# Products of probabilities and values per head pair and key source, key block by key block over all queries

## The chip, the cores and the metric

The kernel runs on one core of a Trainium2 chip. The metric is the time of one execution in device microseconds (us). The median of three runs of the kernel before is 1021.41 us (1021.05 to 1021.64).

## What is computed

One layer of a decoder trunk over 512 positions (four query tiles of 128) with a model width of 1024, in 32-bit floats. After a norm and one combined projection, three attention branches A, B and C run over the same positions, are gated, merged and projected, and a feed-forward part follows. Cut to what matters here:

```
A, B, C:  p = softmax(q @ k^T * scale + bias, causal / selected / windowed)
A:  o = p @ v                                   8 heads, one shared v
B:  o = g0*pc @ vcmp + g1*ps @ vs + g2*pw @ vw   8 heads in 2 groups; gates are folded into p
C:  o = (near p) @ v0 + (two dilated p) @ v1, v2   4 output heads, one common softmax
x = x + (sig(gA)*(oA @ W_a) + sig(gB)*(oB @ W_b) + sig(gC)*(oC @ W_c)) @ W_out
x = x + SwiGLU(norm(x))
```

In B the key sources ps and pw cover the same 512 keys here (si = 0 and 1 in the code), and the compressed source pc has 32 keys.

## The kernel before

TensorE (PE) does everything with matrices. The large products (projections, gates, merges, feed-forward) are split into a rounded high part and a low part and done as three float32r matmuls (L106 to L108, mm3). The attention runs beside them: `tick()` advances a generator that emits one step of a software pipeline between pieces of the projections, and the framework's scheduler then sets each engine's order from emission order and its own estimate. Engines run their own rows in that fixed order.

A unit of A or B is one head pair, one query tile i, and in B one key source si. Its step a computes scores of both heads (lg, L363 and L364), adds the bias table on VectorE (DVE, L531), takes the exponential on ScalarE (ACT, L546) and normalises on DVE (L547, L548). Step b transposes the probabilities p on PE, key block by key block (tr, L111, `transposed`), and ACT copies the result to SBUF as pT (L527). Step c multiplies values and probabilities: for key blocks b_ = 0..i and heads j = 0, 1 one matmul with a 128x64 stationary block of v and 128 moving columns of pT, into rows 64j..64j+63 of the PSUM tile ov (L658, L710, in C L874). A head pair has one ov; B adds two more matmuls per query tile for the compressed source (L662), C adds 32 small ones at the end (L882). `head_out` then splits ov into high and low parts (ACT L81, DVE L82) as the tile oT, from which the merge products read.

Column-split matmuls are those whose stationary block has 64 or 32 columns: the two heads of a pair use the two halves of PE's columns. A plain float32 matmul is two records in the trace; a transpose and a float32r matmul are one.

There are two PSUM tiles for scores (lg), two for transposes (tr), one for ov, three for the large products (pm). `ready(bi)` (L997) calls tick until a branch's four oT tiles exist; while it does, no new gate or merge products are emitted.

Of the kernel before, what the change touches and what calls it, by code (L numbers as in the profile page):

```python
# [11 lines left out]
F32 = mybir.dt.float32  # L12
# [8 lines left out]
S = 512  # L21
D = 1024
NT = S // 128
# [44 lines left out]
def block_kernel(ctx: ExitStack, tc: tile.TileContext, x, norm1_g, norm2_g, w_in, qk_norm_g, cmp_pos, cmp_w,  # L68
                 w_ba, w_bb, w_bc, w_out, w_fi, w_fo, rel_bias, onehot, masks, out):
    nc = tc.nc  # L70
# [448 lines left out]
        proj_tm([(C_BQ + 256 * c, 256)], lambda t, ps: nc.scalar.copy(q_tm[:, t, :], ps[:, 0:256]), then=then)  # L519


    def transposed(p, n):
        ps = tr_tile()
        for b in range(n):
            transpose(ps[:, b, :], p[:, b * 128:(b + 1) * 128])
        pt = ap_.tile([128, 4, 128], F32, name="pT", tag="pT", bufs=6)
        nc.scalar.copy(pt[:, 0:n, :], ps[:, 0:n, :])  # L527
        return pt

    def add_table(dst, lg, tab, init, m):  # L530
        nc.vector.tensor_tensor_reduce(out=dst, in0=lg, in1=tab, scale=-1.0, scalar=init, op0=ALU.add, op1=ALU.min,  # L531
# [53 lines left out]
    def cmp_scores(g):  # L585

        def a():
            lg = lg_tile()
            for j in range(4):
                nc.tensor.matmul(lg[32 * j:32 * j + 32, :], kcs[:, 32 * g:32 * g + 32], bq[4 * g + j].bitcast(F32),  # L590
                                 start=True, stop=True)
            sT = ap_.tile([128, S], F32, name="cmpT", tag="p", bufs=5)
            nc.scalar.copy(sT, lg)
            cs_[g] = sT

        return [a]

    def cmp_unit(g, i):
        d = {}

        def a():
            ps = tr_tile()
            transpose(ps[:, 0, :], cs_[g][:, 128 * i:128 * i + 128])
            lg = ps.rearrange("p k c -> p (k c)")
            p = ab.tile([128, 4, 32], F32, name="pc", tag="pc", bufs=2)
            m = ty.tile([128, 8], F32, name="mc", tag="mc")
            nc.vector.tensor_tensor(out=p, in0=lg[:, 0:128].rearrange("p (h n) -> p h n", n=32),
                                    in1=cmask[:, 32 * i:32 * i + 32].unsqueeze(1).to_broadcast([128, 4, 32]), op=ALU.add)
            nc.vector.tensor_reduce(out=m[:, 0:4], in_=p, op=ALU.max, axis=AX.X)
            nc.vector.tensor_tensor(out=p, in0=p, in1=m[:, 0:4].unsqueeze(2).to_broadcast([128, 4, 32]),  # L610
                                    op=ALU.subtract)
            nc.scalar.activation(p, p, AF.Exp)
            nc.vector.tensor_reduce(out=m[:, 4:8], in_=p, op=ALU.add, axis=AX.X)
            nc.vector.reciprocal(m[:, 4:8], m[:, 4:8])
            nc.vector.tensor_tensor(out=m[:, 4:8], in0=m[:, 4:8], in1=bg4[:, i, 4 * g:4 * g + 4, 0], op=ALU.mult)
            nc.vector.tensor_tensor(out=p, in0=p, in1=m[:, 4:8].unsqueeze(2).to_broadcast([128, 4, 32]), op=ALU.mult)
            d["p"] = p

        def b():
            ps = tr_tile()  # L620
            transpose(ps[:, 0, :], d["p"].rearrange("p h n -> p (h n)"))
            pt = ab.tile([128, 128], F32, name=f"pcT{g}_{i}")
            nc.scalar.copy(pt, ps[:, 0, :])
            pcs[g, i] = pt

        return [a, b]

# [2 lines left out]
    def b_units():  # L630
        for pr in range(4):
            hs = (2 * pr, 2 * pr + 1)
            g = pr // 2
            d = {}
            for i in range(NT):
                for si in range(2):
                    yield b_unit(pr, hs, g, i, si, d)

    def b_unit(pr, hs, g, i, si, d):
        u = {}  # L640
        qcol = slice(i * 128, (i + 1) * 128)

        def a():
            if i == 0 and si == 0:
                d["tab"] = [bias_table(8 + h) for h in hs]
            u["p"] = [causal_probs(bq[h], i, bk[si][g], d["tab"][j], None, bg4[:, i, h, si + 1:si + 2])
                      for j, h in enumerate(hs)]

        def b():
            u["pt"] = [transposed(p, i + 1) for p in u["p"]]  # L650
# [36 lines left out]

    def a_unit(pr, i, d):
        u = {}
        qcol = slice(i * 128, (i + 1) * 128)  # L690

        def a():
            if i == 0:
                d["tab"] = [bias_table(2 * pr + j) for j in range(2)]
            if i == 1 and pr < 3:
                a_load(pr + 1)
            if i == 3 and pr < 3:
                a_query(pr + 1)
            u["p"] = [causal_probs(aq[pr][j], i, st_["ak"], d["tab"][j], topm[i], None) for j in range(2)]

        def b():
            u["pt"] = [transposed(p, i + 1) for p in u["p"]]

        def c():
            if i == 0:
                d["ov"] = pvp.tile([128, S], F32, name="ova", tag="pv")
            ov = d["ov"]
            for b_ in range(i + 1):
                for j in range(2):
                    nc.tensor.matmul(ov[64 * j:64 * j + 64, qcol], av[:, b_, :], u["pt"][j][:, b_, :],  # L710
                                     start=(b_ == 0), stop=(b_ == i))
            if i == NT - 1:
                oA.append(head_out(ov))

        return [a, b, lambda: None, c]


    dC = dp.tile([6, 128, NT, 256], F32, name="dC")
# [95 lines left out]
    def c_unit(hf, i, j, ld, d):  # L814
# [30 lines left out]
        def b():  # L845
            ps = tr_tile()
            p = u["p"]
            for b_ in range(w0 // 128):
                transpose(ps[:, b_, :], p[:, 128 * b_:128 * b_ + 128])
            if i < 2:  # L850
                transpose(ps[:, 2, :], p[:, w0 + 2 * n - 128:w0 + 2 * n])
            else:
                for g in range(2):
                    transpose(ps[0:n, 2 + g, :], p[:, w0 + g * n:w0 + g * n + n])
            pt = ap_.tile([128, 4, 128], F32, name="pT", tag="pT", bufs=6)
            nc.scalar.copy(pt[:, 0:w0 // 128, :], ps[:, 0:w0 // 128, :])
# [6 lines left out]
            d[i, j] = pt  # L863

        def c():
            if j == 0:
                return
            if i == 0:
                d["ov"] = pvp.tile([128, S], F32, name="ovc", tag="pv")
            ov = d["ov"]  # L870
# [5 lines left out]
            if i == NT - 1:  # L876
                ovr = ov.rearrange("p (i r w) -> p r i w", i=NT, r=4)
                for g in (1, 2):
                    for r in range(4):
                        for jj in range(2):  # L880
                            h = slice(64 * jj, 64 * jj + 64)
                            nc.tensor.matmul(ovr[h, r], ld["v", g][:, r, h], ld["pt", jj][:, g - 1, :, 32 * r:32 * r + 32],  # L882
                                             start=False, stop=(g == 2 and r == 3))
                oC.append(head_out(ov, unperm=True))

        return [a, b, c]

    def attention():
        yield from pipeline(ab_units())
# [264 lines left out]
```

## Time and profile before

| what | value |
| --- | --- |
| median of three runs | 1021.41 us |
| the profiled execution | 1021.53 us |
| its span in the trace | 1019.7 us |
| PE busy | 1004.5 us (99%) |
| DVE / ACT / POOL busy | 560.3 / 440.2 / 174.8 us |
| PE clock granted | 1.00 |

The span is the time from the first to the last traced instruction; 1.8 us of the profiled execution lie outside it. A matmul's end is modelled, so on PE the steps from start to start are read, not the durations.

### The profile page before, as it was taken

To read this page: it belongs to the slowest core of one execution; us is meant where nothing else is said; L and a number is where in the kernel's file an instruction comes from. 1 tells how busy PE (TensorE), PEld (TensorE's weight loads), DVE (VectorE), ACT (ScalarE), POOL (GpSimd) and SP (SyncE) were. 2 spreads that over 40 slices of the span, in tenths; PEclk is the share of its full clock that TensorE was granted. 3 is DMA by queue.
4 is the path that set the end of the run, shared out by engine and by line. 5 is a ranking of instruction groups with operands and counts; after the bars stand their busy time and mean duration, and the time that the engine had idled before them with its cause. 6 is when DMAs were issued, how large, how long until landed. Compare 5 with 4: busy or idle time off the path is not lost.

```text
span 1019.7 us, 16838 instructions
## 1 busy us (share of the span) xinstructions
PE 1004.5 (99%) x6247; PEld 847.0 (83%) x6247; DVE 560.3 (55%) x1277; ACT 440.2 (43%) x956; POOL 174.8 (17%) x156
## 2 busy tenths in 40 slices
PE   6999999999999999999999999999999999999998
PEld 6799999798887777777777889998888888888886
DVE  7699998555554565554676554553443443432321
ACT  5544555555555555554553433442332332322220
POOL 4226556234100022221010213100000000000000
PEclk9999999999999999999999999999999999999999
DMA  9442244233132333335742353233243333332421
GB/s 212 111 125 53 80 136 130 83 112 98 61 94 82 84 113 105 99 109 156 213 150 83 103 186 115 84 109 98 83 111 96 85 112 94 89 108 94 137 79 42
DMA packets 119267, 109.96 MB, mean 108 GB/s; under 512 B 19931, under 2 KB 105234, under 8 KB 119186
## 3 DMA queue, kind: packets, MB, share of 16 engines
q1 hardware_dynamic: 116994, 107.85, 36.4%
q10 hardware_dynamic: 2192, 1.05, 0.4%
q8 instruction: 49, 0.80, 0.3%
q14 instruction: 32, 0.26, 0.1%
HBM read 96.66 MB, written 12.21 MB: 107 GB/s over the span
## 4 chain that ended last, share of the span: by engine, by line
PE 93%; DMA 3%; SPq 1%; DVE 1%; issue 1%; ACT 0%; POOL 0%; DVEq 0%; ACTq 0%; POOLq 0%
PE pf L108 13%; PE pf L107 13%; PE pf L106 13%; PE pm L107 12%; PE pm L108 12%; PE pm L106 12%; PE tr L111 5%; PE ovb L658 3%; PE lg L363 2%; PE lg L364 2%; PE ova L710 2%; DMA raw<-in_w_in 1%; SPq L246 1%; PE ovc L874 1%; PE lg L829 1%
## 5 line engine op out<-in xcount | busy, mean ns | idle before, releaser
L82 DVE TENSOR_TENSOR wlo<-raw,whi 128x512 fp32r<-128x512 f32 (+1 forms) x243 | 178.5, 741 | 156.1 <-ACT whi L81 151.5
L81 ACT CAST whi<-raw 128x512 fp32r<-128x512 f32 (+1 forms) x288 | 176.6, 618 | 182.1 <-PE pf L108 78.6
L107 PE MATMUL pm<-wlo,xh 128*128 128x256 f32 (+1 forms) x512 | 145.8, 287 | 0.3 <-DVE wlo L82 0.3
L108 PE MATMUL pm<-whi,xl 128*128 128x256 f32 (+1 forms) x512 | 145.1, 285 | 0.5 <-POOL xl L82 0.5
L106 PE MATMUL pm<-whi,xh 128*128 128x256 f32 (+1 forms) x512 | 144.7, 286 | 0.6 <-ACT bgt L374 0.6
L107 PE MATMUL pf<-xl,whi 128*128 128x512 f32 (+1 forms) x384 | 142.6, 372 | 0.1
L106 PE MATMUL pf<-xh,whi 128*128 128x512 f32 (+1 forms) x384 | 142.5, 372 | 0.0
L108 PE MATMUL pf<-xh,wlo 128*128 128x512 f32 (+1 forms) x384 | 142.0, 371 | 0.0
L107 PEld LDWEIGHTS pm<-wlo,xh 128*128 128x128 f32 x512 | 98.1, 192 | 2.3 <-issue 1.2
L108 PEld LDWEIGHTS pm<-whi,xl 128*128 128x128 f32 x512 | 98.1, 192 | 1.6 <-POOL xl L82 0.8
L106 PEld LDWEIGHTS pm<-whi,xh 128*128 128x128 f32 x512 | 97.8, 192 | 1.1 <-ACT bgt L374 0.9
L106 PE MATMUL pm<-xh,whi 128*128 128x512 f32 x224 | 89.1, 398 | 0.0
L108 PE MATMUL pm<-xh,wlo 128*128 128x512 f32 x224 | 89.1, 398 | 0.0
L107 PE MATMUL pm<-xl,whi 128*128 128x512 f32 x224 | 88.9, 397 | 0.0
L82 POOL TENSOR_TENSOR wlo<-raw,whi 128x512 fp32r<-128x512 f32 x45 | 62.9, 1415 | 130.4 <-ACT whi L81 119.8
L107 PEld LDWEIGHTS pf<-xl,whi 128*128 128x128 f32 x384 | 72.3, 188 | 12.7 <-DVE xl L82 0.3
L108 PEld LDWEIGHTS pf<-xh,wlo 128*128 128x128 f32 x384 | 72.2, 188 | 12.6
L106 PEld LDWEIGHTS pf<-xh,whi 128*128 128x128 f32 x384 | 72.2, 188 | 12.3
L106 PE MATMUL pf<-whi,hh 128*128 128x512 f32 x176 | 69.4, 395 | 0.0
L108 PE MATMUL pf<-whi,hl 128*128 128x512 f32 x176 | 69.4, 395 | 0.0
L107 PE MATMUL pf<-wlo,hh 128*128 128x512 f32 x176 | 69.4, 395 | 0.0
L527 ACT COPY pT<-tr 128x128 f32<-128x128 f32 (+3 forms) x96 | 40.7, 426 | 62.6 <-PE tr L111 62.3
(312 smaller groups left out, 1768.2 us busy)
## 6 DMA issues: line engine op xcount, KB each, us to landing
raw<-in_w_in SPq DMA_DIRECT2D x92, 256.0 KB, 3.1
raw<-in_w_ffn_in SPq DMA_DIRECT2D x88, 256.0 KB, 2.8
raw<-in_w_ffn_out SPq DMA_DIRECT2D x44, 256.0 KB, 2.7
raw<-in_w_in SPq DMA_DIRECT2D x52, 128.0 KB, 2.5
x<-in_x SPq DMA_DIRECT2D x8, 512.0 KB, 5.8
tab<-dvec SPq DMA_DIRECT2D x16, 256.0 KB, 3.4
dz<-tz SPq DMA_DIRECT2D x16, 256.0 KB, 2.9
tz<-dz SPq DMA_DIRECT2D x16, 256.0 KB, 2.9
```

What stands on the lines that cost most here:

```text
L81: nc.scalar.copy(dst_hi, src)
L82: (eng or nc.vector).tensor_tensor(out=dst_lo, in0=src, in1=dst_hi.bitcast(F32), op=ALU.subtract)
L106: nc.tensor.matmul(ps, ah, bh, start=(j == 0), stop=False)
L107: nc.tensor.matmul(ps, ah, bl, start=False, stop=False)
L108: nc.tensor.matmul(ps, al, bh, start=False, stop=(j == n - 1))
L111: nc.tensor.transpose(dst, src, ident[0:src.shape[0], 0:src.shape[0]])
L246: nc.sync.dma_start(dst, src)
L363: nc.tensor.matmul(lg, qs, k[:, 0, 0:w], start=True, stop=False)
L364: nc.tensor.matmul(lg, qs, k[:, 1, 0:w], start=False, stop=stop)
L527: nc.scalar.copy(pt[:, 0:n, :], ps[:, 0:n, :])
L658: nc.tensor.matmul(ov[64 * j:64 * j + 64, qcol], bv[si][:, b_, 64 * g:64 * g + 64], u["pt"][j][:, b_, :], start=(si == 0 and b_ == 0), sto ...
L710: nc.tensor.matmul(ov[64 * j:64 * j + 64, qcol], av[:, b_, :], u["pt"][j][:, b_, :], start=(b_ == 0), stop=(b_ == i))
```

## The change

Step c of A, B and C runs once per key source of a head pair, after the last query tile's probabilities have been copied, and not per query tile. For each key block b it multiplies the value block with all queries from tile b on: 512, 384, 256 and 128 moving columns for b = 0..3 (in C 256, 256, 256 and 128). For that the transposed probabilities of all four query tiles lie in one tile per head (13 blocks of 128x128, in C 7), ordered so that the blocks of one key block are neighbours; the copy L530 writes block by block into it. There are four such tiles where there were six of four blocks. In B the loop over key sources is now outside the loop over query tiles, and the compressed probabilities of a group are one tile, so that their product is one matmul of 512 columns per head. The scratch for descriptors of dynamic DMAs is set to 1024 bytes; the kernel's own DMAs are issued from SP and ACT.

```diff
-    def transposed(p, n):
+    def pt_tile(n):
+        return ap_.tile([128, n, 128], F32, name="pT", tag="pT", bufs=4)
+    def transposed(pt, p, i):
         ps = tr_tile()
-        for b in range(n):
+        for b in range(i + 1):
             transpose(ps[:, b, :], p[:, b * 128:(b + 1) * 128])
-        pt = ap_.tile([128, 4, 128], F32, name="pT", tag="pT", bufs=6)
-        nc.scalar.copy(pt[:, 0:n, :], ps[:, 0:n, :])
-        return pt
+        nc.scalar.copy(pt[:, i:4 * i + 1:3, :], ps[:, 0:i + 1, :])
+    def weighted_values(ov, v, pts, first, last):
+        for b in range(NT):
+            for j in range(2):
+                nc.tensor.matmul(ov[64 * j:64 * j + 64, 128 * b:S], v(b), pts[j][:, 4 * b:3 * b + NT, :],
+                                 start=first and b == 0, stop=last and b == NT - 1)
...
-            for i in range(NT):
-                for si in range(2):
+            for si in range(2):
+                for i in range(NT):
                     yield b_unit(pr, hs, g, i, si, d)
...
         def c():
-            if i == 0 and si == 0:
+            if si == 0:
                 d["ov"] = pvp.tile([128, S], F32, name="ovb", tag="pv")
             ov = d["ov"]
-            for b_ in range(i + 1):
-                for j in range(2):
-                    nc.tensor.matmul(ov[64 * j:64 * j + 64, qcol], bv[si][:, b_, 64 * g:64 * g + 64],
-                                     u["pt"][j][:, b_, :], start=(si == 0 and b_ == 0), stop=False)
+            weighted_values(ov, lambda b_: bv[si][:, b_, 64 * g:64 * g + 64], u["pt"], si == 0, False)
             if si == 1:
                 for j in range(2):
-                    nc.tensor.matmul(ov[64 * j:64 * j + 64, qcol], vcp[:, hs[j], :], pcs[g, i], start=False, stop=True)
-                if i == NT - 1:
-                    oB.append(head_out(ov))
-        return [a, b, c]
+                    nc.tensor.matmul(ov[64 * j:64 * j + 64, :], vcp[:, hs[j], :], pcs[g].rearrange("p i q -> p (i q)"),
+                                     start=False, stop=True)
+                oB.append(head_out(ov))
+        return [a, b, c] if i == NT - 1 else [a, b]
...
-        return [a, b, lambda: None, c]
+            ov = pvp.tile([128, S], F32, name="ova", tag="pv")
+            weighted_values(ov, lambda b_: av[:, b_, :], d["pt"], True, True)
+            oA.append(head_out(ov))
+        return [a, b, lambda: None, c] if i == NT - 1 else [a, b]
...
-            for b_ in range(w0 // 128):
-                for jj in range(2):
-                    h = slice(64 * jj, 64 * jj + 64)
-                    nc.tensor.matmul(ov[h, 128 * i:128 * i + 128], ld["v", 0][:, k0 // 128 + b_, h], d[i, jj][:, b_, :],
-                                     start=(i == 0 and b_ == 0), stop=False)
+            for b_ in (0, 2, 1, 3):
+                q1 = min(b_ + 2, NT)
+                for jj, h in enumerate(hs):
+                    nc.tensor.matmul(ov[h, 128 * b_:128 * q1], ld["v", 0][:, b_, h], d["pt", jj][:, 2 * b_:b_ + q1, :],
+                                     start=b_ == 0, stop=False)
...
-    nc = bacc.Bacc("TRN2", target_bir_lowering=False, num_devices=1)
+    nc = bacc.Bacc("TRN2", target_bir_lowering=False, num_devices=1, dynamic_dma_scratch_size=1024)
```

The new names are L530 (copy of pT), L536 (`weighted_values`), L540 and L555 (table and exponential), L670 (compressed source), L876 (C).

PE, end of branch B before (lg_4509 and later are the first scores of A; p_4442 and p_4451 are the last probabilities of B):

```order
L111 MATMUL tr_4491<-ident_82,p_4442 128x128 x4
L363 MATMUL lg_4509<-kst_823,qst_4477 128x128
L364 MATMUL lg_4509<-kst_823,qst_4477 128x128
L111 MATMUL tr_4498<-ident_82,p_4451 128x128 x4
L658 MATMUL ovb_4121<-pT_4496,bv1_888 64x128
L363 MATMUL lg_4518<-kst_823,qst_4480 128x128
L364 MATMUL lg_4518<-kst_823,qst_4480 128x128
L363 MATMUL lg_4562<-kst_823,qst_4477 128x256
L364 MATMUL lg_4562<-kst_823,qst_4477 128x256
L111 MATMUL tr_4552<-ident_82,p_4512 128x128
L658 MATMUL ovb_4121<-pT_4503,bv1_888 64x128
L658 MATMUL ovb_4121<-pT_4496,bv1_888 64x128
```

The same place on PE now (p_4278 and p_4287 are the last probabilities of B, lg_4275 and lg_4284 their scores four rows further up, aq_in the queries of A):

```order
L111 MATMUL tr_4228<-ident_82,p_4181 128x128 x2
L111 MATMUL tr_4265<-ident_82,p_4235 128x128 x3
L111 MATMUL tr_4270<-ident_82,p_4244 128x128 x3
L111 MATMUL tr_4308<-ident_82,aq_in_4263 128x128 x4
L111 MATMUL tr_4319<-ident_82,p_4278 128x128 x4
L111 MATMUL tr_4325<-ident_82,p_4287 128x128 x4
L536 MATMUL ovb_4152<-pT_4161,bv1_888 64x512
L363 MATMUL lg_4335<-kst_823,qst_4313 128x128
L364 MATMUL lg_4335<-kst_823,qst_4313 128x128
L536 MATMUL ovb_4152<-pT_4162,bv1_888 64x512
L536 MATMUL ovb_4152<-pT_4161,bv1_888 64x384
L536 MATMUL ovb_4152<-pT_4162,bv1_888 64x384
```

Six groups of transposes now follow each other with no other product between them; one product of 512 columns stands alone, and the other seven of the key source and the two compressed ones follow in one stretch.

ACT at that place before (the last exponentials of B stand eight rows further up):

```order
L527 COPY pT_4437<-tr_4432 128x512
L320 ACTIVATE qst_4477<-tr_4472,gain8_91 64x512
L320 ACTIVATE qst_4480<-tr_4472,gain8_91 64x512
L527 COPY pT_4496<-tr_4491 128x512
L546 ACTIVATE p_4512,m_4513<-p_4512,m_4513 128x128
L527 COPY pT_4503<-tr_4498 128x512
```

ACT there now, from the last exponentials of B on:

```order
L555 ACTIVATE p_4278,m_4279<-p_4278,m_4279 128x512
L530 COPY pT_4161<-tr_4265 128x3x128
L555 ACTIVATE p_4287,m_4288<-p_4287,m_4288 128x512
L530 COPY pT_4162<-tr_4270 128x3x128
L320 ACTIVATE qst_4313<-tr_4308,gain8_91 64x512
L530 COPY pT_4161<-tr_4319 128x4x128
L320 ACTIVATE qst_4316<-tr_4308,gain8_91 64x512
L530 COPY pT_4162<-tr_4325 128x4x128
```

The exponentials, the copies and A's first queries now alternate, and each copy frees one of the two tr tiles. ACT's rows are the same in number as before.

PE at the end of branch A now (p_5254 and p_5265 are the last probabilities of A):

```order
L363 MATMUL lg_5260<-kst_823,qst_5000 128x512
L364 MATMUL lg_5260<-kst_823,qst_5000 128x512
L111 MATMUL tr_5244<-ident_82,p_5218 128x128 x3
L111 MATMUL tr_5287<-ident_82,p_5254 128x128 x4
L111 MATMUL tr_5293<-ident_82,p_5265 128x128 x4
L536 MATMUL ova_5377<-pT_5137,av_248 64x512
L111 MATMUL tr_5408<-ident_82,c_in_5283 128x128 x4
L536 MATMUL ova_5377<-pT_5138,av_248 64x512
```

Here too no large product stands between the last scores and the transposes that need them. Before, between the same scores (lg_5495) and their transposes there were 21 large products (pm_5830, pm_5909), of which the first six stand here:

```order
L363 MATMUL lg_5495<-kst_823,qst_5217 128x512
L364 MATMUL lg_5495<-kst_823,qst_5217 128x512
L108 MATMUL pm_5830<-oT_4870,wlo_5727 128x512
L106 MATMUL pm_5830<-oT_5147,whi_5726 128x512
L107 MATMUL pm_5830<-oT_5147,whi_5726 128x512
L108 MATMUL pm_5830<-oT_5147,wlo_5727 128x512
L106 MATMUL pm_5830<-oT_5419,whi_5732 128x512
L107 MATMUL pm_5830<-oT_5419,whi_5732 128x512
L111 MATMUL tr_5478<-ident_82,p_5448 128x128 x3
```

The large products that filled this piece of PE's row now stand ahead of it.

Over the whole order, PE's products of probabilities and values (L658, L662, L710, L874, L882) stood in 108 unbroken stretches, 332 matmuls in all; now (L536, L670, L876, L882) they stand in 36, with 152 matmuls.

## Rows read from the trace of the kernel before

**Rows 1.** The page: PE's busy time, and the chain by engine.
```profile
PE 1004.5 (99%) x6247; PEld 847.0 (83%) x6247; DVE 560.3 (55%) x1277; ACT 440.2 (43%) x956; POOL 174.8 (17%) x156
...
PE 93%; DMA 3%; SPq 1%; DVE 1%; issue 1%; ACT 0%; POOL 0%; DVEq 0%; ACTq 0%; POOLq 0%
```
**Rows 2.** Windows of B, A, C: length, busy PE, PEld, DVE, ACT, POOL; clock, DMA.
```profile
180.00:358.00 178.00, 177.14 (x1345) 149.11 (x1344) 98.09 (x305) 99.10 (x266) 32.07 (x24) 1.00 0.29 86
358.00:467.00 109.00, 108.91 (x601) 81.84 (x601) 59.72 (x159) 55.95 (x132) 24.25 (x24) 1.00 0.39 113
467.00:566.00 99.00, 98.02 (x753) 73.79 (x754) 60.88 (x162) 46.20 (x97) 11.50 (x9) 1.00 0.47 140
```
**Rows 3.** PE's groups by line and shape: busy, mean ns | idle.
```profile
L658 PE MATMUL ovb<-pT,bv 128*64 128x128 f32 x320 | 36.8, 286 | 0.0
...
L662 PE MATMUL ovb<-pcT,vcp 128*64 128x128 f32 x64 | 9.7, 276 | 0.0
...
L710 PE MATMUL ova<-pT,av 128*64 128x128 f32 x160 | 18.9, 290 | 0.0
...
L874 PE MATMUL ovc<-pT,c_v 128*64 128x128 f32 x56 | 7.6, 292 | 0.0
```
**Rows 4.** Timeline of PE (start, duration) around a stretch of one matmul.
```profile
462.32 0.40 PE L107 MATMUL pm<-xl,whi 128*128 128x512 f32 x1
462.65 0.43 PE L710 MATMUL ova<-pT,av 128*64 128x128 f32 x2
463.01 0.66 PE L111 MATMUL tr<-ident,c_in 128*128 128x128 f32 x4
463.43 0.47 PE L108 MATMUL pm<-xh,wlo 128*128 128x512 f32 x1
463.74 0.39 PE L106 MATMUL pm<-xh,whi 128*128 128x512 f32 x1
463.97 0.40 PE L107 MATMUL pm<-xl,whi 128*128 128x512 f32 x1
```
**Rows 5.** Timeline of PE around a stretch of seven matmuls.
```profile
465.22 1.09 PE L710 MATMUL ova<-pT,av 128*64 128x128 f32 x14
466.24 0.66 PE L111 MATMUL tr<-ident,c_in 128*128 128x128 f32 x4
```
**Rows 6.** Timeline of PE around L590 (512 columns, 32-column blocks): four matmuls, then one.
```profile
127.92 1.07 PE L590 MATMUL lg<-qst,kcs 128*32 128x512 f32 x8
128.91 0.39 PE L107 MATMUL pm<-wlo,xh 128*128 128x256 f32 x1
...
182.49 1.05 PE L590 MATMUL lg<-qst,kcs 128*32 128x512 f32 x2
183.47 0.43 PE L658 MATMUL ovb<-pT,bv 128*64 128x128 f32 x2
```
**Rows 7.** Chain of waits: four transposes in a row (start, time).
```profile
476.24 0.44 PE tr L111 x4
```
**Rows 8.** ACT's groups by line and shape: busy, mean ns | idle, releaser.
```profile
L546 ACT ACTIVATE p<-p,m 128x512 f32<-128x512 f32 x24 | 17.3, 720 | 7.9 <-DVE m L531 7.9
...
L527 ACT COPY pT<-tr 128x512 f32<-128x512 f32 x24 | 14.1, 587 | 18.6 <-PE tr L111 18.5
L527 ACT COPY pT<-tr 128x384 f32<-128x384 f32 x24 | 11.5, 478 | 15.9 <-PE tr L111 15.8
...
L320 ACT ACTIVATE qst<-tr,gain 64x512 fp32r<-64x512 f32 x16 | 10.9, 684 | 9.6 <-DVE qst L321 7.3 <-PE tr L111 2.1
```
**Rows 9.** Timeline: from a pair's last scores to its probabilities, 512 columns.
```profile
340.86 0.39 PE L364 MATMUL lg<-kst,qst 128*128 128x512 f32 x1
...
343.32 0.55 DVE L548 TENSOR_SCALAR p<-p,m,bgt 128x512 f32<-128x512 f32 x1
```
**Rows 10.** Waits of PE and of its weight loads: total, times, longest.
```profile
PEld tr L111 <- issue: 11.0, 62, 0.5
...
PEld ovb L658 <- issue: 6.1, 31, 0.4
...
PE tr L111 <- ACT pT L527: 0.8, 1, 0.8
```

More of the change, by code (lines that the diff above doesn't have):

```diff
@@ L594, in a @@
             cs_[g] = sT
+            pcs[g] = ab.tile([128, NT, 128], F32, name=f"pcT{g}")
         return [a]
@@ L621, in b @@
             transpose(ps[:, 0, :], d["p"].rearrange("p h n -> p (h n)"))
-            pt = ab.tile([128, 128], F32, name=f"pcT{g}_{i}")
-            nc.scalar.copy(pt, ps[:, 0, :])
-            pcs[g, i] = pt
+            nc.scalar.copy(pcs[g][:, i, :], ps[:, 0, :])
         return [a, b]
@@ L640, in b_unit @@
         u = {}
-        qcol = slice(i * 128, (i + 1) * 128)
         def a():
@@ L649, in b @@
         def b():
-            u["pt"] = [transposed(p, i + 1) for p in u["p"]]
+            if i == 0:
+                d["pt"] = [pt_tile(13) for _ in hs]
+            for j, p in enumerate(u["p"]):
+                transposed(d["pt"][j], p, i)
+            u["pt"] = d["pt"]
         def c():
-            if i == 0 and si == 0:
+            if si == 0:
                 d["ov"] = pvp.tile([128, S], F32, name="ovb", tag="pv")
             ov = d["ov"]
-            for b_ in range(i + 1):
-                for j in range(2):
-                    nc.tensor.matmul(ov[64 * j:64 * j + 64, qcol], bv[si][:, b_, 64 * g:64 * g + 64],
-                                     u["pt"][j][:, b_, :], start=(si == 0 and b_ == 0), stop=False)
+            weighted_values(ov, lambda b_: bv[si][:, b_, 64 * g:64 * g + 64], u["pt"], si == 0, False)
             if si == 1:
                 for j in range(2):
-                    nc.tensor.matmul(ov[64 * j:64 * j + 64, qcol], vcp[:, hs[j], :], pcs[g, i], start=False, stop=True)
-                if i == NT - 1:
-                    oB.append(head_out(ov))
-        return [a, b, c]
+                    nc.tensor.matmul(ov[64 * j:64 * j + 64, :], vcp[:, hs[j], :], pcs[g].rearrange("p i q -> p (i q)"),
+                                     start=False, stop=True)
+                oB.append(head_out(ov))
+        return [a, b, c] if i == NT - 1 else [a, b]
     dA = dp.tile([2, 128, NT, 256], F32, name="dA")
@@ L689, in a_unit @@
         u = {}
-        qcol = slice(i * 128, (i + 1) * 128)
         def a():
@@ L701, in b @@
         def b():
-            u["pt"] = [transposed(p, i + 1) for p in u["p"]]
+            if i == 0:
+                d["pt"] = [pt_tile(13) for _ in range(2)]
+            for j, p in enumerate(u["p"]):
+                transposed(d["pt"][j], p, i)
         def c():
[L705 to L713, printed above, removed]
-        return [a, b, lambda: None, c]
+            ov = pvp.tile([128, S], F32, name="ova", tag="pv")
+            weighted_values(ov, lambda b_: av[:, b_, :], d["pt"], True, True)
+            oA.append(head_out(ov))
+        return [a, b, lambda: None, c] if i == NT - 1 else [a, b]
     dC = dp.tile([6, 128, NT, 256], F32, name="dC")
@@ L854, in b @@
                     transpose(ps[0:n, 2 + g, :], p[:, w0 + g * n:w0 + g * n + n])
-            pt = ap_.tile([128, 4, 128], F32, name="pT", tag="pT", bufs=6)
-            nc.scalar.copy(pt[:, 0:w0 // 128, :], ps[:, 0:w0 // 128, :])
+            if i == 0:
+                d["pt", j] = pt_tile(7)
+            lo_ = max(2 * i - 1, 0)
+            nc.scalar.copy(d["pt", j][:, lo_:2 * i + 1, :], ps[:, 0:w0 // 128, :])
             if i < 2:
@@ L862, in b @@
                 nc.vector.tensor_copy(ld["pt", j][0:n, :, i, :], ps[0:n, 2:4, :])
-            d[i, j] = pt
         def c():
[L866 to L870, printed above, removed]
-            for b_ in range(w0 // 128):
-                for jj in range(2):
-                    h = slice(64 * jj, 64 * jj + 64)
-                    nc.tensor.matmul(ov[h, 128 * i:128 * i + 128], ld["v", 0][:, k0 // 128 + b_, h], d[i, jj][:, b_, :],
-                                     start=(i == 0 and b_ == 0), stop=False)
[L876 to L886, printed above, removed]
+            ov = pvp.tile([128, S], F32, name="ovc", tag="pv")
+            hs = [slice(64 * jj, 64 * jj + 64) for jj in range(2)]
+            for b_ in (0, 2, 1, 3):
[3 more added lines that the diff above has]
+                                     start=b_ == 0, stop=False)
+            ovr = ov.rearrange("p (i r w) -> p r i w", i=NT, r=4)
+            for g in (1, 2):
+                for r in range(4):
+                    for jj, h in enumerate(hs):
+                        nc.tensor.matmul(ovr[h, r], ld["v", g][:, r, h], ld["pt", jj][:, g - 1, :, 32 * r:32 * r + 32],
+                                         start=False, stop=(g == 2 and r == 3))
+            oC.append(head_out(ov, unperm=True))
+        return [a, b, c] if i == NT - 1 and j == 1 else [a, b]
     def attention():
```

## The prediction

> **What bounds the kernel now.** I read the page first: PE is busy for 1004.5 of 1019.7 us, and 93% of the chain that ended last is PE [rows 1]. In the windows of the three branches PE is busy all but 0.9, 0.1 and 1.0 us while DVE and ACT stay at about half, and the granted clock is 1.00 throughout [rows 2]. So a microsecond that leaves PE's row leaves the time, unless it returns as a wait. The groups by line show what the change touches: 320 + 64 + 160 + 56 records of products with probabilities [rows 3], two for each float32 matmul. Their busy times contain modelled ends, so I read prices from starts in the timeline.
>
> **Price of a stretch.** The groups cannot show what a change between full and column-split matmuls costs; the timeline does. From 462.32 to 463.97 PE issues two large products, one lone matmul of probabilities, four transposes and one more large product [rows 4]: 1.65 us. A large product among its like takes 0.23 (463.74 to 463.97). Four transposes in a row take 0.44 [rows 7], and two records of the lone matmul take 0.22 (below). That makes 3 x 0.23 + 0.44 + 0.22 = 1.35. The remaining 0.30 us is the price of one stretch of column-split matmuls: the wait before its first weights, its start, and the wait and start of what follows.
>
> **Price of the columns.** A lone matmul of 128 columns takes 0.36 from its start to the next (462.65 to 463.01) [rows 4]. A stretch of seven takes 1.02 (465.22 to 466.24) [rows 5]. It begins with the second head, which has four of the seven; if the two heads' halves run side by side it is eight records long. The difference of six records is 0.66, so a record of 128 columns costs 0.11 and 0.14 of the 0.30 lies inside the stretch. That 14 records fit into 1.02 shows that the halves do run side by side. The nearest rows for 512 columns are those of L590, four 32-column blocks at once: four matmuls take 0.99, one alone takes 0.98 [rows 6]. Less 0.14 that is two records of 0.425, the same per column as 0.11 per 128. So longer matmuls gain next to nothing by themselves, and one of 512 columns that stands alone occupies PE as long as a full pair.
>
> **The change, part by part.**
>
> *Stretches.* 108 become 36. 72 x 0.30 = 21.6 us go. With prices of 0.28 to 0.34 (large products behind a stretch lose a little more than transposes) it is 20.2 to 24.5.
>
> *Columns.* The sum of columns is unchanged. Perfectly paired, before would be 332 / 2 x 0.22 = 36.5 us. Counted stretch by stretch with the fuller half of each it is 46.7, because 47 or so matmuls stand unpaired. Now the ideal is about 35.5, but in each of the eight passes of B, four pairs of A and two halves of C one head's first matmuls stand alone ahead of the rest: 14 x 0.85 = 11.9, together 47.5. That is 0.8 us more. Two halves with matmuls of unequal length, as in the new stretches (512 beside 384 columns), do not occur in this trace. Below, nothing can beat the fuller half; above, the halves would run one after the other and the columns would cost up to twice as much. I take the fuller half, the row that it is nearest to being L590, whose four blocks overlap wholly.
>
> *L590 and C's scores.* In the order L590 is in two stretches instead of three; the lone one at 182.49 goes: 0.98 + 0.16 of the outer price, 1.1 us less. C's small score products stand in one stretch more: 0.3.
>
> *Wait at the end of B.* With query tiles 0 to 3 of the last source in a row, `ready(1)` has six groups of transposes on PE with no large product between. ACT serves them in series: from the exponential of p_4278 to the copy that frees the tile for tr_4325 it has 0.72 + 0.48 + 0.72 + 0.48 + 0.68 + 0.59 = 3.67 us [rows 8]. PE has tr_4270, tr_4308 and tr_4319 meanwhile, 11 transposes of 0.11, 1.2 us. So PE idles some 2.5 us; before, the same place cost 0.8 [rows 10]. Plus 1.7.
>
> *Wait at the end of A.* From the start of a pair's last score matmul to normalised probabilities 3.0 us pass (340.86 to 343.32 + 0.55) [rows 9]. Between lg_5260 and tr_5293 PE now has the rest of that matmul and seven transposes, 1.0 us. Plus 2.0, where the 21 large products covered it before. The head_out that follows is as late against its readers as before and costs nothing new.
>
> *The rest costs nothing.* ACT, DVE and POOL have as many rows as before; the copies of pT write the same elements in 512-byte pieces. Elsewhere in the order over 1.2 us of PE work stand between a pair's last transposes and its products, more than a copy of 0.59; if that cover failed, each of the 14 passes could lose up to that much. Four pT tiles suffice, since a source's two are read one step before the second next source asks for them. The smaller DMA scratch touches no queue that the kernel fills.
>
> The sum: -21.6 + 0.8 - 1.1 + 0.3 + 1.7 + 2.0 = -17.9. The profiled execution took 1021.53, which is 0.12 above the median of the runs and 1.8 above its span; with what lies outside the span unchanged this gives 1003.6, and **1003.5 us** as a median.
>
> **A rule against the trace.** Eight records of 128 columns and two of 512 columns take 1.02 and 0.99 [rows 5, 6]: six records fewer save 0.03. The Trainium skill, "TensorEngine Tiling (Array Packing)", section Performance Considerations, says that each matmul on this chip has about 60 cycles of overhead, so that long matmuls are worth more than their columns. By that rule 180 matmuls fewer would save, as an estimate from that page's figure at 2.4 GHz, 25 ns each, 4.5 us, and the time would be near 999. The rows leave no room for it in this form of matmul.
>
> **Rivals.**
>
> *The halves do not overlap (slower).* If two heads with 512 and 384 columns, accumulating into one ov tile, run one after the other, the columns cost 47.5 us twice. The place is L536; the price is up to 47.5, and from 18 us, some 38% of it, the change is slower than before. At full price: 1003.5 + 47.5 = 1051. For it: no such pair in the trace, and L590 does not accumulate. Against: the stretch of seven accumulates and overlaps [rows 5], L590 overlaps at 512 columns [rows 6]. Chance 0.03.
>
> *The gain returns as waits.* In B and A three of four pipeline steps now have no product of probabilities, so PE has less to do between scores and transposes. If each of the 12 sources of A and B idles 0.7 us more, 8.4 us return: 1012. For it: the two places above. Against: ACT and DVE are at 55% in B's window [rows 2], and the order has large products between scores and transposes everywhere else. Chance 0.10.
>
> *A stretch is cheaper than read.* The weight loads' idle time before transposes is 11.0 us in 62 cases, 0.18 each, 0.20 for L658 [rows 10]. If only 0.18 can be saved, 72 x 0.18 = 13.0 us go: 1012. Against: the 1.65 us of rows 4 hold 0.30 that nothing else explains. Chance 0.07.
>
> *Long matmuls are faster than their columns.* If 512 columns cost 0.23 a record, as for a large product [rows 4], and not 0.425, the columns halve: 1003.5 - 22 = 982. Against: rows 6 show 0.425. Chance 0.03. The page's rule above would be a small form of this, inside the range.
>
> *The stretches are not fewer.* The order is that of the program that will run, so I give this nothing.
>
> **How the numbers follow.** The forecast has 0.77. Its own range is 996 to 1010: the low end takes 24.5 for the stretches and no waits, the high end 20.2 and 5 us more of waits than I counted. The two rivals at 1012 lie just outside; half of each reaches in when the range ends at 1011. So 996 to 1011 holds a little over 0.8. Faster by over 0.2% (2 us, about what a measurement of this kernel can tell from no change) are the forecast and all rivals but the first, less a tail of the waits: 0.95. Within 0.2%: 0.02, the far end of the waits. Slower: 0.03.
>
> **What would show it.** In the profile after: a record of 512 columns of L536 in steps of 0.42 to 0.43 in pairs of heads at once, a whole pass of B's first source about 0.99 for the lone matmul and 2.28 for the other seven; weight loads of transposes waiting on issue in far fewer than 62 cases; PE's busy windows of B, A and C together about 20 us shorter; two new waits of PE for ACT or DVE at the ends of B and A of 2 to 2.5 us; columns of L106 to L108 unchanged. The prediction is wrong if a pass of seven takes over 3 us, or if waits of PE on L111 and L536 add up to more than 10 us.

## The result, and the profile after

The changed kernel takes 1009.71 us (median of 4 runs, 1007.56 to 1011.72) against 1021.52 us before: a ratio of 0.9884, 95% interval 0.9862 to 0.9905. It is faster by 11.8 us. That is inside the predicted range, and 6.2 us short of the forecast of 1003.5. A second series of 4 runs gave 1009.88 us (0.9877, 0.9860 to 0.9893). The profile shown here is of an execution of 1011.72 us, with a span of 1009.9.

PE's busy time and the chain, which answer to [rows 1], and one group of PE by line and shape, which answers to [rows 3]:

```profile
PE 989.5 (98%) x5887; PEld 831.6 (82%) x5887; DVE 566.1 (56%) x1277; ACT 439.4 (44%) x956; POOL 176.7 (17%) x156
...
PE 90%; DMA 3%; SPq 3%; DVE 1%; issue 1%; ACT 1%; POOL 0%; DVEq 0%; POOLq 0%
```

```profile
L536 PE MATMUL ovb<-pT,bv 128*64 128x512 f32 x32 | 17.7, 637 | 0.0
```

PE still bounds the kernel, with 15.0 us less of busy time. But the span fell by 9.8 only: PE now sits idle for 20.4 us of it, before for 15.2. Where that is, the waits of PE in branches B to C show (total, times, longest):

```profile
PE tr L111 <- DVE m L556: 2.3, 1, 2.3
PE tr L111 <- ACT pT L530: 1.5, 3, 0.5
PE tr L111 <- DVE p L557: 0.9, 1, 0.9
PE tr L111 <- DMA c_in<-dC: 0.7, 1, 0.7
PE tr L111 <- DVE qst L321: 0.7, 1, 0.7
```

Before, the same windows had one wait of 0.8 us for ACT [rows 10] and two for c_in, 0.8 together. The new ones add up to 6.1 us, and all but the one for c_in lie at the two places that the prediction named. The end of A, on PE (start, duration, idle time before it):

```profile
444.47 0.40 PE L364 MATMUL lg<-kst,qst 128*128 128x512 f32 x1
447.15 0.52 PE L111 MATMUL tr<-ident,p 128*128 128x128 f32 x3 [2.29 <-DVE m L556]
448.22 0.63 PE L111 MATMUL tr<-ident,p 128*128 128x128 f32 x4 [0.54 <-ACT pT L530]
449.77 1.09 PE L111 MATMUL tr<-ident,p 128*128 128x128 f32 x4 [0.92 <-DVE p L557]
450.79 1.97 PE L536 MATMUL ova<-pT,av 128*64 128x512 f32 x2
452.68 1.11 PE L111 MATMUL tr<-ident,c_in 128*128 128x128 f32 x4
453.73 3.36 PE L536 MATMUL ova<-pT,av 128*64 128x512 f32 x14
457.02 0.66 PE L111 MATMUL tr<-ident,c_in 128*128 128x128 f32 x4
```

Two things are to be seen. PE idles for 2.29 + 0.54 + 0.92 us. And what comes then is slow: the lone matmul takes 1.89 from start to start (450.79 to 452.68), four transposes 1.05, the other seven matmuls 3.29, where undisturbed ones take 0.99 [rows 6], 0.44 [rows 7] and 2.3 (below). The windows of 5 us name the reason in the third column from the end, the granted clock:

```profile
445.00:450.00 5.00, 1.38 (x8) 0.99 (x9) 3.72 (x7) 1.98 (x5) 1.80 (x3) 0.84 0.59 176
450.00:455.00 5.00, 5.00 (x14) 2.19 (x15) 0.00 (x0) 0.59 (x1) 0.00 (x0) 0.50 0.39 115
455.00:460.00 5.00, 4.76 (x23) 2.72 (x20) 2.12 (x4) 2.84 (x5) 0.00 (x0) 0.89 0.81 232
```

After 3.6 us of idle in one window PE runs at 0.50, that is 1.2 instead of 2.4 GHz; in the same branches before, the clock was 1.00 [rows 2]. From 444.47 to 457.02 pass 12.55 us for records that at full clock and without a wait take 5.15 (0.23 + 11 x 0.11 + 0.99 + 0.44 + 2.28). So the end of A costs 7.4 us in this execution. What held PE up is on DVE and POOL in the same stretch:

```profile
444.11 2.90 DVE L557 TENSOR_SCALAR p<-p,m 128x384 f32<-128x384 f32 x1
```

```profile
444.06 2.74 POOL L815 MEMSET pt<- 128x1024 f32 x3
```

A scale of 128x384 that takes 0.41 us elsewhere (at 441.24) takes 2.90, and ends 0.2 us after the three memsets of POOL. The kernel before had the same memsets beside DVE, in a place where little of DVE's work met them (its timeline of DVE, then of POOL):

```profile
450.98 0.69 DVE L531 CUSTOM_DVE_ANT_0 p<-lg,tabm 128x512 f32<-128x512 f32 x1 [0.27 <-PE lg L364]
...
452.76 0.91 DVE L548 TENSOR_SCALAR p<-p,m 128x512 f32<-128x512 f32 x1
```

```profile
450.43 2.95 POOL L811 MEMSET pt<- 128x1024 f32 x3
```

There the same kind of scale took 0.91 instead of 0.49, ending just after the memsets, and the score operation, which reads PSUM, ran beside them at its usual 0.69. The Trainium skill, SBUF — State Buffer, section SBUF: two separate sides, says that some DVE operations and GpSimd share a pair of ports which whoever starts first holds, while the other blocks. Both traces agree: the scale, from SBUF to SBUF, waits out POOL; the operation on PSUM does not.

### The profile page after: what moved, and what is told of

It reads as the page before. It is cut to its first block, busy times and chain, and to the rows that moved or that the text cites. A ratio compares the mean times of both kernels' runs of the same rounds, so it can differ in the third digit from the quotient of the medians.

```text
span 1009.9 us, 16083 instructions
## 1 busy us (share of the span) xinstructions
PE 989.5 (98%) x5887; PEld 831.6 (82%) x5887; DVE 566.1 (56%) x1277; ACT 439.4 (44%) x956; POOL 176.7 (17%) x156
## 3 DMA queue, kind: packets, MB, share of 16 engines
q10 hardware_dynamic: 2192, 1.05, 0.4%
## 4 chain that ended last, share of the span: by engine, by line
PE 90%; DMA 3%; SPq 3%; DVE 1%; issue 1%; ACT 1%; POOL 0%; DVEq 0%; POOLq 0%
PE pf L108 14%; PE pf L107 14%; PE pf L106 14%; PE pm L106 12%; PE pm L108 12%; PE pm L107 12%; PE tr L111 4%; PE ovb L536 3%; PE lg L363 2%; PE lg L364 2%; SPq L246 1%; PE ova L536 1%; DMA raw<-in_w_in 1%; DMA tz<-dz 1%; DMA c_in<-dC 1%
## 5 line engine op out<-in xcount | busy, mean ns | idle before, releaser
L82 DVE TENSOR_TENSOR wlo<-raw,whi 128x512 fp32r<-128x512 f32 (+1 forms) x243 | 180.9, 748 | 145.1 <-ACT whi L81 143.8
L555 ACT ACTIVATE p<-p,m 128x128 f32<-128x128 f32 (+3 forms) x96 | 53.9, 562 | 36.8 <-DVE m L540 35.3
```

Source lines behind the costliest of these rows:

```text
L82: (eng or nc.vector).tensor_tensor(out=dst_lo, in0=src, in1=dst_hi.bitcast(F32), op=ALU.subtract)
L555: nc.scalar.activation(p[:, 0:w], p[:, 0:w], AF.Exp, bias=m[:, 0:1], scale=-1.0, accum_out=m[:, 1:2])
```

## The experiments

All are edits of the changed kernel, which ran again on the same chip as the first three. The others ran on two more chips; the kernel before took 1022.13, 1021.54 and 1021.28 us on the three.

**The changed kernel again.** 

> The changed kernel once more, beside the others on the same chip, so that they are compared with it and not only with the kernel before. Expected: 1009.7 us within 2, and at the end of A the same picture: the scale of 128x384 on DVE (L557) near 2.9 us while POOL writes zeros to pt12 (L815), PE idle for some 5 us between 445 and 450, and the granted clock near 0.5 right behind. If the long scale was a chance of one execution, it reads 0.5 us here.

1009.88 us; the profiled execution took 1011.39. The long scale is there again (2.91), so is the idle time at the end of A. The clock was 0.85 and 0.81 in the windows from 445 and 450, and this time it fell behind the end of B too (0.66 from 340 to 344; 0.95 in the first profile, as nearly everywhere in that one). The 8 executions of the kernel spread over 4 us, and apart from the first profiled one, where the clock reads 0.946, time follows the mean granted clock: 1007.56 at 0.998, 1011.39 at 0.994. The 0.95 of that one does not show in PE's pace: from 556 to 700 us it has 921 records in 143.87 us of busy time, the repeated profile at 1.00 has 921 in 143.84.

**The memset on VectorE.**

```diff
-            nc.gpsimd.memset(pt, 0.0)
+            nc.vector.memset(pt, 0.0)
```

> One line: the zeroing of pt12 (L815) is issued on VectorE instead of GpSimd, behind the last normalisation of A; the order of PE is that of the changed kernel (36 column-split stretches). Theory (the end of A was mis-sized because POOL's three memsets lie beside DVE's L557 and stretch it from 0.5 to 2.9 us, and the longer gap then lets PE's clock fall): L557 takes 0.5 to 0.6 us there, PE waits there for about 2 us instead of 5, the granted clock behind it falls less or not at all, and the time is 3 to 5 us below the changed kernel, 1005 to 1007. Rival one (the wait is the chain's own length, and POOL only fills it): L557 stays over 2 us or another step takes its place, time within 1 us of the changed kernel. Rival two (the wait goes, but the clock falls all the same): 2 to 2.5 us less, about 1007.5, with a window of granted clock near 0.5 behind the end of A.

1009.6 us: no gain that stands out of the scatter (four executions from 1006.68 to 1011.02), although the end of A is mended. On PE there:

```profile
443.82 0.63 PE L111 MATMUL tr<-ident,p 128*128 128x128 f32 x4 [1.06 <-DVE p L557]
444.99 0.63 PE L111 MATMUL tr<-ident,p 128*128 128x128 f32 x4 [0.54 <-DVE p L557]
445.54 1.07 PE L536 MATMUL ova<-pT,av 128*64 128x512 f32 x2
446.55 0.66 PE L111 MATMUL tr<-ident,c_in 128*128 128x128 f32 x4
447.13 2.37 PE L536 MATMUL ova<-pT,av 128*64 128x512 f32 x14
449.43 0.66 PE L111 MATMUL tr<-ident,c_in 128*128 128x128 f32 x4
```

The scale takes 0.42, PE idles 1.6 us instead of 3.75, and the lone matmul (1.01) and the seven (2.30) run at full clock; A's last product starts 5 us earlier than in the repeated run. So the memsets on POOL are the cause of the long wait. But the waits of PE as a whole show where the gain went:

```profile
PE tr L111 <- DMA c_in<-dC: 2.6, 1, 2.6
PE tr L111 <- DVE p L557: 1.6, 2, 1.1
PE lg L828 <- DVE cks L771: 1.2, 1, 1.2
```

The start of C is late instead: its first scores wait 1.2 us for the split keys, and a transpose 2.6 us for a load of c_in (none and 1.6 in the repeated run). Behind both the clock falls: 0.75 from 455 to 460, 0.50 from 482 to 488. Rival one had the time right and the mechanism wrong: it was not another step at A's end that took the place, but two of the next branch.

**The heads swapped.**

```diff
-            for j in range(2):
+            for j in (1, 0):
...
-                for jj, h in enumerate(hs):
+                for jj, h in reversed(list(enumerate(hs))):
```

> The two heads of a pair change places in the products of the changed kernel (the second head's matmul of a key block is written ahead of the first's). In the order the lone first matmul is gone then: 21 column-split stretches instead of 36, and 14 matmuls of 512 columns no longer stand alone. Theory (a stretch costs 0.30 us, a lone first matmul holds PE for 0.85 us that its partner could have shared): 15 x 0.30 + 11.1 us of columns = 15.6 us less than the changed kernel, 994, if nothing comes back as a wait; up to 3 us of waits for the second head's copy may come back, since no stretch starts before both copies are there: 994 to 997. Rival one (a stretch is cheaper, 0.18 us): 2.7 + 11.1 = 13.8 less, 996 to 999. Rival two (a pass takes as long as it does whatever its order, the halves share less than read): within 4 us of the changed kernel.

995.04 us, 0.9731 of before (0.9714 to 0.9747), 14.8 us below the changed kernel; expected were 15.6 less up to 3. It is the best version of all. A pass of B in it:

```profile
285.21 2.37 PE L536 MATMUL ovb<-pT,bv 128*64 128x512 f32 x16
287.51 0.55 PE L111 MATMUL tr<-ident,p 128*128 128x128 f32 x3
```

All eight matmuls take 2.30 us in one stretch. In the changed kernel the lone one (1.0) came on top of 2.3 for the other seven: the first matmul's partner rides free. This bears out the price of columns by the fuller half. The 15 stretches alone do not tell 0.30 from 0.18 us, since 1.8 us is less than the scatter. The kernel before does: against it the swapped one has 87 stretches fewer (108 to 21), 10.3 us less of columns (46.7 to 47.5 - 11.1) and 0.8 less for L590 and C's scores. At 0.18 that would be 26.8 us, of which 6.3 come back as waits of PE in B to C (1.6 before, 7.9 now). Measured are 27.1, so 0.18 is too little.

The end of A is not mended in this version either. PE waits 2.89 us there behind a scale of 3.82 us beside POOL, the clock reads 0.50 from 435 to 440, and from the last scores to the transposes behind A's last product (430.87 to 442.90) 12 us pass.

**Branch A per query tile again.** Step c of A with its old loops (i, key block, head; 128 columns) on the new tiles; B and C unchanged.

> Branch A alone is undone: its products run per query tile again, in 128 columns, from the new tiles of pT; B and C stay as changed. The order has 63 column-split stretches instead of 36, about the same columns, and large products between the last transposes of A again. Theory (the end of A lost 7.8 us in the changed kernel: wait 5, clock 3): 27 stretches x 0.30 = 8.1 us more and some 6 to 7.8 us less at the end of A, time 1010 to 1012, no idle stretch of PE over 1 us between 440 and 460 and no clock of 0.5 there. Rival one (the loss is spread over the passes of B and A, not at A's end): 8 us more than the changed kernel, 1017 to 1018. Rival two (a stretch is cheaper than 0.30 us, which is why the changed kernel gained less than forecast): 27 x 0.18 = 4.9 more and 6 to 7.8 less, 1007 to 1009.

1013.78 us, 3.9 more than the changed kernel. The scale beside the memsets takes 3.12 us here too, and costs nothing: between 430 and 470 the profile shows no wait of PE at all, since large products stand before the transposes, and the clock stays at 1.00. The theory expected 1010 to 1012, the rival of spread loss 1017 to 1018; the time misses the first by 1.8 us and is far from the second. If the end of A gave back 6.1 to 7.4 us (below), the 27 stretches more cost 10 to 11, not the 8.1 of the theory. The place is shown, the size only to within 3 us.

**Pieces of 128 columns.**

```diff
-                nc.tensor.matmul(ov[64 * j:64 * j + 64, 128 * b:S], v(b), pts[j][:, 4 * b:3 * b + NT, :],
-                                 start=first and b == 0, stop=last and b == NT - 1)
+                for t in range(b, NT):
+                    nc.tensor.matmul(ov[64 * j:64 * j + 64, 128 * t:128 * t + 128], v(b), pts[j][:, 3 * b + t, :],
+                                     start=first and b == 0 and t == 0, stop=last and b == NT - 1)
```

> The passes of the changed kernel stay where they are, but weighted_values issues every product in pieces of 128 columns (20 matmuls a pass instead of 8), as the kernel before did. The order then has 74 column-split stretches instead of 36, since large products and scores come between the pieces, and about 4 us less of columns by the fuller half. Theory (the price is that of the stretch, 0.30 us, and a matmul of 512 columns costs what four of 128 cost): 38 x 0.30 - 4.3 = 7 us more than the changed kernel, 1017 +- 1.5; within an undisturbed pass two records of 128 columns of both heads step 0.22 a pair, 0.11 a record. Rival (a record has a cost of its own beside its columns): pairs of 128 columns step clearly above a quarter of the 0.85 of a pair of 512, and the time is above 1019. The Trainium skill, TensorEngine Tiling (Array Packing), section Performance Considerations, has some 60 cycles for each matmul; by that, as an estimate from that page, another 4 us would come on top.

1014.67 us, 4.8 above the changed kernel and 2.3 below what I expected. I had left out that this order, too, relieves the end of A: its longest wait there is 0.64 us, and the clock stays at 1.00. Against that, its columns are only 2 us less by the fuller half (46.9 against 48.8 when both orders are counted at 0.22 a pair), not 4. A stretch of it:

```profile
311.83 1.59 PE L537 MATMUL ovb<-pT,bv 128*64 128x128 f32 x24
313.20 0.59 PE L671 MATMUL ovb<-pcT,vcp 128*64 128x512 f32 x1
...
314.43 0.55 PE L111 MATMUL tr<-ident,p 128*128 128x128 f32 x3
```

24 records of both heads take 1.37 us (to 313.20), 0.114 for a pair of 128 columns. Whole, to the transposes behind it, the stretch takes 2.60 us; its fuller half is 14 records of 128 columns and two of 512, as much as 22 such pairs, which is 0.118 each. The pass of the swapped kernel shown above, measured in the same way, has 16 records of 512 to 128 columns, as much as 20 such pairs, and takes 2.30, which is 0.115 each. So a matmul has next to no cost beside its columns. The rule of the Trainium skill, TensorEngine Tiling (Array Packing), section Performance Considerations, on an overhead for each matmul is not borne out as a cost on top of the columns.

**C's loads on ScalarE.** The memset on VectorE, and:

```diff
-            nc.sync.dma_start(t_, dC[n, :, :, c0:c0 + 128])
+            (nc.scalar if hf else nc.sync).dma_start(t_, dC[n, :, :, c0:c0 + 128])
```

> The kernel with the zeroing of pt12 on VectorE, and besides the six loads of c_in for the second half of C (L745) issued by ScalarE instead of SyncE. In the run before this one the end of A was 4 us shorter and the time was the same: PE then waited 2.6 us for a c_in load that stood on SP's queue behind 14 loads of ctab. Theory (SP's queue gives the gain back): the wait of transposes for c_in falls from 2.6 us to under 0.8, and the time from 1009.6 to 1006 to 1007.5. Rival one (the transfer itself is late because the 16 DMA engines are full of tables): the load is issued earlier and lands no earlier, 1009 to 1010. Rival two (PE waits next for the chain of transposes, copies and splits behind it): the c_in wait goes and one of the same size stands on lg or tr behind ACT or DVE, 1009 to 1010.

1006.33 us, 3.3 less than with the memset alone (the executions of the two overlap) and 3.5 less than the changed kernel. The time is as the theory had it, the wait is not:

```profile
PE tr L111 <- DMA c_in<-dC: 1.7, 1, 1.7
```

1.7 us are left of 2.6, not under 0.8. ScalarE issued the load at 476.31, SyncE at 476.75 in the run before: it too was waiting there, by the profile for a table (ctab). Clock is a rival: it stays at 1.00 behind the wait (479 to 485), where it was 0.50 with the memset alone; the four executions read 0.998, those with the memset alone 0.994 to 0.998, and the one of those at 0.998 took 1006.68, within the range of these four. That SP's queue alone gave the gain back is therefore not shown.

**The gap filled.** Twelve records of score matmuls, whose results nothing uses, before the transposes that wait:

```diff
+            if pr == 3 and i == NT - 1:
+                for _ in range(6):
+                    qk(lgs[-2], aq[pr][0], i, st_["ak"])
```

> The changed kernel with 12 score matmuls of 512 columns repeated into a score tile that has been read, between the last score of A and the transposes that wait for DVE; their results are used by nothing. They are 2.8 us of work in a gap of 2.5 us; all else stands in the order as before. Theory (PE's idle time is what lets its clock fall): the granted clock stays at or near 1.00 from 445 to 455, four transposes take 0.44 instead of 0.7 to 1.0 and the lone first matmul 0.99 instead of 1.9, and the time is 1.5 to 3 us below the changed kernel, 1007 to 1008.5, unless the start of C gives a part back. Rival (the clock falls for what stays there, two waits of 0.7 and 1.1 us and the pass itself): the clock falls all the same and the time is 0.3 us above the changed kernel.

1007.61 us, 2.3 less with more work on PE, though the executions overlap (1005.41 to 1009.54, the repeated run from 1008.56). The windows from 445 on, and the last passes:

```profile
445.00:450.00 5.00, 4.15 (x25) 2.31 (x25) 0.91 (x3) 2.24 (x5) 0.00 (x0) 1.00 0.51 152
450.00:455.00 5.00, 4.75 (x24) 2.94 (x20) 3.09 (x5) 3.54 (x6) 0.91 (x1) 1.00 0.86 239
```

```profile
447.13 1.07 PE L536 MATMUL ova<-pT,av 128*64 128x512 f32 x2
448.14 0.66 PE L111 MATMUL tr<-ident,c_in 128*128 128x128 f32 x4
448.72 2.37 PE L536 MATMUL ova<-pT,av 128*64 128x512 f32 x14
```

The clock stays at 1.00 and the passes take 1.01 and 2.30. So in this execution PE's idle time is what the clock had fallen for. Of the four executions two had a clock of 1.000 and took 1005.41 and 1005.84, two had 0.997 and took 1009.38 and 1009.54: the end of B still leaves PE idle. Where the clock fell in the two slower ones, which have no profile, is not known.

**Three edits together**: heads swapped, memset on VectorE, C's loads on ScalarE. 

> Three edits together on the changed kernel: heads swapped in the products, the zeroing of pt12 on VectorE, the second half's c_in loads issued by ScalarE. 21 column-split stretches. The swapped heads alone gave 995.0. If the two others add what their theory has (3 us at the end of A, nothing given back at the start of C): 991 to 993. Rival (the other chains at the start of C take it back, as with the memset alone): 994.5 to 996.

997.22 us: a miss, 2.2 above the swapped heads alone. PE waited 5.8 us for c_in, and its clock was 0.51 and 0.50 from 470 to 480. The next run parts the edits.

**Heads swapped and memset on VectorE.** 

> The heads swapped and the zeroing of pt12 on VectorE, the loads of c_in on SyncE as in the changed kernel. It parts the two edits of the run with all three (997.2 us, where PE waited 5.8 us for a c_in load issued by ScalarE and its clock stood at 0.51 for 10 us behind that). Theory (the loads on ScalarE were the harm there, held up in ScalarE's own order): the wait for c_in is under 3 us and the time 992 to 995. Rival (C starts too early for its loads, whoever issues them): a wait for c_in of 4 us or more and 996 to 998.

997.08 us, so the rival holds. PE and the windows behind it:

```profile
466.56 0.40 PE L828 MATMUL lg<-cks,cqs 128*128 128x256 f32 x2
471.64 1.11 PE L111 MATMUL tr<-ident,c_in 128*128 128x128 f32 x4 [4.69 <-DMA c_in<-dC]
```

```profile
470.00:475.00 5.00, 3.36 (x28) 2.13 (x31) 0.61 (x3) 1.63 (x3) 0.00 (x0) 0.50 0.91 253
475.00:480.00 5.00, 5.00 (x28) 3.86 (x28) 4.35 (x14) 2.78 (x6) 0.00 (x0) 0.50 0.75 235
```

C now comes before its loads, whichever engine issues them. The chain of waits runs over the values and loads ahead in the queue, in order of time:

```profile
456.38 6.36 DMA c_v<-dV
...
468.02 3.58 DMA c_in<-dC
```

The transposes behind A's last product start at 438.58, 4.3 us earlier than with the swapped heads alone (442.90); that is lost again here, as a wait and as ten microseconds of half clock.

**Heads swapped and the gap filled.** 

> The heads swapped in the products, and the 12 idle score matmuls of 512 columns in the gap at the end of A; their results are used by nothing. The two edits alone gave 995.0 and 1007.6, 14.8 and 2.3 us below the changed kernel. If they concern different things (the columns and stretches of the passes, the clock at the end of A) they add up: 992 to 994, with a granted clock near 1.00 between 430 and 445. Rival (the start of C takes the second gain back, in its wait for c_in): 994.5 to 996.

996.92 us: no gain over 995.04, and no test of the sum. With the heads swapped the order puts three transposes, which wait for the long scale, ahead of the twelve records, so PE idled 2.9 us as before and did the idle work on top. The edit missed its place.

No run undoes the new loop order of B, the four larger pT tiles or the smaller DMA scratch by themselves; what each of them costs or gives is not shown.

## Why the prediction was right, and where it was off

*The bound.* Right: PE's row is the time, and what left it left the time, less the new waits. The measured time lies 1.3 us inside the upper end of the range, in room that was left for waits in general and not for what came.

*Stretches and columns.* Right as far as the runs tell: 15 stretches and 11.1 us of columns less brought 14.8 of 15.6 us, and a lone first matmul and the seven behind it measure 1.0 and 2.3 as forecast. PE's weight loads before transposes wait on issue in 20 cases, not 62 [rows 10], but for 16.6 us in all and not 11.0, with single waits of up to 2.7. One number in the working is wrong: in the order before, 96 matmuls stand unpaired, not 47. The sum of 46.7 does not hang on it; counted again it is 47.1. The windows of B, A and C together are 366 us long (190 to 556) instead of 386; half of that is only B's later first product, so this sign was badly chosen.

*The halves overlap, long matmuls cost their columns.* Right; both rivals fall with the 2.30 us of a whole pass.

*The end of B.* Forecast 2.5 us of idle, found:

```profile
336.75 1.40 PE L111 MATMUL tr<-ident,p 128*128 128x128 f32 x8
338.68 0.66 PE L111 MATMUL tr<-ident,aq_in 128*128 128x128 f32 x4 [0.53 <-ACT pT L530]
339.76 0.67 PE L111 MATMUL tr<-ident,p 128*128 128x128 f32 x4 [0.42 <-ACT pT L530]
341.11 0.66 PE L111 MATMUL tr<-ident,p 128*128 128x128 f32 x4 [0.68 <-DVE qst L321]
341.70 1.10 PE L536 MATMUL ovb<-pT,bv 128*64 128x512 f32 x2
```

The marked waits are 1.6 us. From start to start, 336.75 to 341.70, PE takes 4.95 us for 20 transposes, which at 0.11 each take 2.2: 2.7 us are lost for the 2.5 forecast. Two of the three marked waits are for ACT, which serves the groups in series; the last is for DVE, which reads A's first queries from the tile of transposes (L321). The mechanism is right.

*The end of A: the term that was mis-sized.* "Plus 2.0" stood there; it is 7.4 us in the first profile (idle and half clock, above) and 6.1 in the repeated one (443.43 to 454.65, 11.2 us against 5.15). The step that failed took 3.0 us from the last scores to the probabilities out of [rows 9], a place in B, for the chain at A's end, where it took 5.2 (444.47 to 449.62). That chain shares DVE with POOL's memsets (+2.4 us), which in the trace of before end some 12 us ahead of A's last product; and it assumed that what follows a wait runs as it did before, but the clock falls. The runs confirm both parts one at a time, in one profile each. With the memset moved, the scale takes 0.42 and the same stretch 7.4 us (442.03 to 449.43), 2.2 more than 5.15: the 2.0 of the forecast. With the gap filled and the memsets in place, the clock stays at 1.00 and 4.2 us are lost (441.65 to 451.02 against 5.15). So of the 7.4 us about 2 are the wait that was forecast, 2 the memsets and 3 the clock. The 4.2 are 2.2 more than forecast, and 1003.5 + 2.2 = 1005.7 is near what the two executions at full clock took. The rest of the way to 1009.7 is clock, and waits at the start of C: the repeated profile has a lowered clock behind the end of B (0.66 from 340 to 344), the end of A (0.81 from 450 to 455) and a wait for c_in (0.57 from 486 to 490). Which part is which differs between executions and is not settled.

*The sign for a wrong forecast* (a pass of seven over 3 us) came true once, for another reason than overlap: the 3.29 us are that pass at half clock. The other sign did not: waits on L111 and L536 in B to C are 6.1 us.

## What to carry to other kernels

Where work that is batched moves to the end of a phase, price the end of the phase by its own chain, with all that other engines do beside it at that moment, and price an idle gap of PE of several microseconds above its length, for the clock behind it (here 3.75 us of idle became 7.4 and 6.1 us). A gain at one wait counts only if the next phase's loads are early enough to use it: moving the memset mended the end of A and met the start of C, alone and with the heads swapped. When two half-width streams share PE, start with the one whose data comes last, so that no matmul stands alone.

## Not expected of the hardware

PE's clock fell to 0.50 behind idle times of 2.6 to 5.8 us, for up to ten microseconds (0.50 from 470 to 480 behind the wait of 4.69). Behind shorter ones it did not fall each time: behind the same three waits at the end of B it read 0.66 (340 to 344) in one profile and 1.00 in that of the filled gap. The Trainium skill, TensorE: Matmul & The Clock Gate, Part 1, tells of a monitor of PE's activity that halves its clock; the runs agree, and add that one kernel's executions differ by 4 us with it. And DVE's scale stood still for all three memsets in a row, 2.90 instead of 0.41 us, not for one of them; with the heads swapped it took 3.82.
